# RWKV-7 scan: v and u as one 128-row operand, decay as a diagonal among the keys, transposes of 128 rows

## The chip, the cores and the metric

The kernel runs on one core of a Trainium2 chip. The metric is the device time of one execution, in microseconds (us). The time before is the median of three runs. The engines are PE (matrix products; PEld is its weight load), DVE, ACT and POOL (element-wise work), and SP, whose queue issues most DMAs. PE writes to PSUM, from which ACT and DVE copy to SBUF.

## What is computed

Two requests, of 256 and 1024 tokens, go through two layers with the same weights: a bidirectional RWKV-7 time mixer, a neighbourhood attention, and a squared-ReLU MLP behind each. The change concerns the recurrence of the time mixer alone, for each of 16 heads (of size 64) and both directions:

```python
def step(S, inp):
    r_t, w_t, k_t, v_t, a_t, b_t = inp
    sa = jnp.einsum('bhvk,bhk->bhv', S, a_t)
    S = S * w_t[:, :, None, :] + sa[..., None] * b_t[:, :, None, :] + v_t[..., None] * k_t[:, :, None, :]
    return S, jnp.einsum('bhvk,bhk->bhv', S, r_t)
```

The results of both directions are added, normalised per head, scaled by `lnx_g`, and a bonus (a number per token and head, times v) is added.

## The kernel before

**Stages.** Projections and preparation (up to about 700 us), the scan (up to about 1360), then gate and output product, MLP, attention and MLP. In the preparation, keys and queries of each chunk of 64 tokens are multiplied by running decays and stored in `x_d`, four arrays per direction: b and k (the "keys"), a and r (the "queries"). `dall` keeps each chunk's total decay, and `v_d` the values, token by token.

**The scan by chunks.** 64 tokens are one chunk, so a step of the scan is a handful of 64x64 products in place of 64 steps of the recurrence. A job is 16 chunks of two heads (e = 0, 1, on partitions 0 to 63 and 64 to 127; `HALVES` gives es, the head's own half, and eo, the other one), in both directions d: at step i the forward chunk i and the backward chunk 15 - i are processed together. Ten jobs of 16 steps make 160 steps. Each product below is done for four units (two directions, two heads); in float32 a product takes two PE instructions. Two steps alternate between two sets of PSUM banks.

**The order is written out by hand.** `at(t, f)` puts a piece of work at time t, counted in steps; all pieces are sorted by t and emitted in that order, and PE, ACT, DVE and POOL run them in that order (`manual_schedule`, line 807). Negative times are work for a later job, done beside the steps of the one before it. SP's DMAs are issued in their order too, each when its buffer is free.

**One step** (`scan_step`, line 1016; all its products are recorded at line 1018), with S the state, A, sn, Y and U areas in PSUM:
- s0n, s0a, s0y (about -0.7 to -0.6, so during the step before): what v contributes to the new state, to A and to Y. They need nothing of the state.
- s1y, s1a (0): S times the queries, added to Y and A. s1c (0.1): ACT copies A to `up`.
- s2 (0.3): `up` times the inverse Q, to U. s2c (0.38): ACT copies U to `u`.
- s2b (0.41): the old S is added to sn through a product with the identity.
- s3n, s3y (0.58): what u contributes to the new state and to Y.
- s3c (0.66): ACT copies sn to the new S, multiplied by the chunk's decay, in one instruction per direction (line 1095).
- s4 (1.15): ACT copies Y out (lines 1100, 1103); in the second half of a job, DVE adds it to the other direction's.

So the next step hangs on S - s1a - `up` - s2 - `u` - s3n - S.

**Beside the steps:** `kprod` (line 973) multiplies the keys by the queries, two chunks of both heads a step, into `kps` (two banks, one buffer); next to the queries a, r in the x tile stands an identity (its fifth array), so that the keys come out transposed too. `kcopy` (ACT) takes these as `ll`, `kmask` (DVE) multiplies the rest by a triangular mask as `zz`. `kload` (line 964) loads an x tile (512 KB) from `x_d` into one of eight buffers. `early`, `keep`, `store`, `rank1` (DVE, many small row updates), `merge1`, `merge2` and the `qd` DMAs make the inverse Q of a later job. `vload` loads v of a job. `scan_post` normalises a finished half of a job (DVE, ACT, POOL), transposes it (`tr`, 16 products of 64x64 a half, into two PSUM banks), copies it (`p5`) and stores it to `z_d`.

Of the kernel before, what the change touches and what calls it, by code (L numbers as in the profile page):

```python
# [13 lines left out]
P = 128  # L14
# [4 lines left out]
L = 64  # L19
# [42 lines left out]
class Trunk:  # L62
# [706 lines left out]
    def scan(self):  # L769
# [32 lines left out]
        self.b_x, self.b_y = ([self.pw.tile([P, 512], F32, name=f"{nm}{i}") for i in range(2)] for nm in ("bx", "by"))  # L802
# [16 lines left out]
    def scan_job(self, j):  # L819
# [113 lines left out]
        for n, (d, g) in enumerate(order):  # L933
# [33 lines left out]
            at(2 * n - 10.0, kload)  # L967

        for q in range(16):
# [3 lines left out]
            def kprod(c, g=g, d=d, pr=pr):  # L973
# [3 lines left out]
                for e, (es, eo) in enumerate(HALVES):  # L977
                    for b, out in ((1, eo), (0, es)):
                        w = 128 if b == 0 else 192
                        mm(J["kp"][out, e, 192 * c + 192 - w:192 * c + 192], x[es, b, 2 * pr + c], x[es, 5 - w // 64:5, 2 * pr + c], start=True, stop=True)  # L980

            def kmask(g=g, d=d, pr=pr):
                J["zz", d, g, pr] = z = self.rp.tile([P, 2, 2, P], F32, name="zz", tag="zz", bufs=8)
# [3 lines left out]
            def kcopy(g=g, d=d, pr=pr):  # L987
                J["ll", d, g, pr] = z = self.rp.tile([P, 2, 2, 64], F32, name="ll", tag="ll", bufs=8)
# [3 lines left out]
            for dt, f in ((0.7, lambda f=kprod: f(0)), (0.72, lambda f=kprod: f(1)), (0.95, kmask), (0.74, kcopy)):  # L992
                at(t + dt, f)
# [22 lines left out]
    def scan_step(self, at, J, st, grp, k, i, new, end):  # L1016
# [10 lines left out]
        def banks():  # L1027
            x, y = self.b_x[k % 2], self.b_y[k % 2]
            return pair(x), pair(y), pair(x[:, P:2 * P]), pair(y[:, P:2 * P])
# [23 lines left out]
        def s1a(d, g, c, cc, e, es, eo, yd):  # L1053
            A, Y, sn, U = banks()
            mm(A[es, d], J["x", d, g][es, 2, c], R["S"][es, d], False, True)

        def s1y(d, g, c, cc, e, es, eo, yd):
            A, Y, sn, U = banks()
            mm(Y[eo, yd], J["x", d, g][es, 3, c], R["S"][es, d], False, False)

        def s1c():
            A, Y, sn, U = banks()
# [3 lines left out]
        def s2(d, g, c, cc, e, es, eo, yd):  # L1066
            A, Y, sn, U = banks()
            mm(U[es, d], J["Q"][es, cc, d], R["up"][es, d], False, True)

        def s2b():  # L1070
            A, Y, sn, U = banks()
            S = R["S"]
            if S is None or end:
                return
            for es, eo in HALVES:
                mm(sn[es], self.ident[es, es], S[es], False, False)

        def s2c():
            A, Y, sn, U = banks()
            R["u"] = self.sp.tile([P, 2, 64], F32, name="u", tag="u", bufs=1)  # L1080
            nc.scalar.copy(R["u"], U)

        def s3n(d, g, c, cc, e, es, eo, yd):
            A, Y, sn, U = banks()
            mm(sn[es, d], ll(d, g, c, e)[es], R["u"][es, d], False, True)

        def s3y(d, g, c, cc, e, es, eo, yd):
            A, Y, sn, U = banks()
            mm(Y[eo, yd], zz(d, g, c, e)[es, 64:128], R["u"][es, d], False, True)

        def s3c():
            A, Y, sn, U = banks()
            S = st["S"] = self.sp.tile([P, 2, 64], F32, name="S", tag="S", bufs=2)
            for d, g, c, cc, m, ch in dirs:
                nc.scalar.activation(S[:, d], sn[:, d], AF.Copy, scale=self.dall[:, m, d, ch:ch + 1])

        def s4():
            A, Y, sn, U = banks()
# [12 lines left out]
        if not end:  # L1111
# [912 lines left out]
```

## Time and profile before

| | us |
|---|---|
| time, median of 3 runs (4079.05 to 4081.42) | 4080.91 |
| the profiled execution | 4071.59 |
| its span, first to last instruction | 4069.7 |
| granted TensorE clock, mean of the span | 0.958 |

The profile is of one execution. A row of a group gives line, engine, operation, out<-in by the program's names (`by<-up,qq` is s2, `bx<-u,ll` s3n, `by<-u,zz` s3y, `bx<-S,x` s1a, `bx<-vv,ll` s0n, `by<-vv,zz` s0y, `bx<-S,cst` s2b), the shape, and the count behind x; then busy time and the mean in ns of one; then the idle time of the engine just before, with what ended it. A row of the timeline gives the start and duration in us. A row of a window gives its bounds and length, the busy time (and count) of PE, PEld, DVE, ACT and POOL, the granted clock, the DMA share and GB/s. "Issue" is time in which an engine waited for nothing that the profile shows. A matmul's duration runs to its last result, so those of neighbours overlap.

### The profile page before, as it was taken

To read this page: it belongs to the slowest core of one execution; us is meant where nothing else is said; L and a number is where in the kernel's file an instruction comes from. 1 tells how busy PE (TensorE), PEld (TensorE's weight loads), DVE (VectorE), ACT (ScalarE), POOL (GpSimd) and SP (SyncE) were. 2 spreads that over 40 slices of the span, in tenths; PEclk is the share of its full clock that TensorE was granted. 3 is DMA by queue.
4 is the path that set the end of the run, shared out by engine and by line. 5 is a ranking of instruction groups with operands and counts; after the bars stand their busy time and mean duration, and the time that the engine had idled before them with its cause. 6 is when DMAs were issued, how large, how long until landed. Compare 5 with 4: busy or idle time off the path is not lost.

```text
span 4069.7 us, 87778 instructions
## 1 busy us (share of the span) xinstructions
PE 3719.3 (91%) x35572; PEld 3101.6 (76%) x35572; DVE 2470.3 (61%) x4771; ACT 1538.8 (38%) x3751; POOL 1308.4 (32%) x1256
## 2 busy tenths in 40 slices
PE   7888979677777799999999989999989999999999
PEld 4665659566666688888888879777768788888888
DVE  7898973466666457555555561567664755555555
ACT  6776652354545441111112132556654211112111
POOL 5450001133334434222222250445553422222222
PEclk8997889799999899999999999999989999999999
DMA  3326655866665431011111115233343111111101
GB/s 110 91 83 214 210 190 158 221 182 180 178 172 135 130 111 37 32 42 42 37 37 42 42 62 176 78 89 82 71 117 130 47 42 42 37 37 42 42 32 63
DMA packets 384005, 393.27 MB, mean 97 GB/s; under 512 B 161873, under 2 KB 306481, under 8 KB 382321
## 3 DMA queue, kind: packets, MB, share of 16 engines
q1 hardware_dynamic: 327728, 307.82, 26.3%
q10 hardware_dynamic: 46704, 61.35, 4.4%
q0 software_dynamic: 9168, 18.49, 1.6%
q8 instruction: 279, 4.57, 0.5%
q14 instruction: 126, 1.02, 0.1%
HBM read 277.54 MB, written 121.24 MB: 98 GB/s over the span
## 4 chain that ended last, share of the span: by engine, by line
PE 71%; DVE 12%; issue 5%; ACT 5%; DMA 4%; POOL 2%; SPq 0%; ACTq 0%; DVEq 0%; POOLq 0%
PE ps L108 17%; PE ps L109 17%; PE ps L110 17%; PE by L1018 3%; PE kps L980 3%; PE bx L1018 3%; PE vps L530 1%; PE vps L531 1%; PE vps L532 1%; PE op L1938 1%; DVE mu L199 1%; DVE ll L287 1%; PE pt L1880 1%; DVE cs L646 1%; PE yps L940 1%
## 5 line engine op out<-in xcount | busy, mean ns | idle before, releaser
L1485 DVE TENSOR_TENSOR x<-ps,x 128x256 f32<-128x256 f32 x1488 | 813.1, 595 | 608.5 <-PE ps L110 608.3
L103 POOL TENSOR_TENSOR wlo<-raw,whi 128x1024 fp32r<-128x1024 f32 (+1 forms) x178 | 391.0, 2196 | 857.0 <-ACT whi L102 812.4
L108 PE MATMUL ps<-ahs,whi 128*128 128x512 f32 x1536 | 613.1, 399 | 0.0
L109 PE MATMUL ps<-als,whi 128*128 128x512 f32 x1536 | 599.3, 390 | 0.0
L110 PE MATMUL ps<-ahs,wlo 128*128 128x512 f32 x1536 | 598.9, 390 | 0.0
L108 PE MATMUL ps<-hh,whi 128*128 128x512 f32 (+1 forms) x1536 | 544.1, 354 | 13.5 <-DVE x L1485 13.5
L109 PE MATMUL ps<-hl,whi 128*128 128x512 f32 (+1 forms) x1536 | 543.2, 354 | 0.0
L110 PE MATMUL ps<-hh,wlo 128*128 128x512 f32 (+1 forms) x1536 | 543.1, 354 | 0.0
L102 ACT CAST whi<-raw 128x1024 fp32r<-128x1024 f32 (+1 forms) x206 | 201.4, 978 | 692.6 <-PE ps L109 632.3
L108 PEld LDWEIGHTS ps<-ahs,whi 128*128 128x128 f32 x1536 | 288.9, 188 | 62.2 <-issue 6.9
L110 PEld LDWEIGHTS ps<-ahs,wlo 128*128 128x128 f32 x1536 | 288.4, 188 | 62.0
L108 PEld LDWEIGHTS ps<-hh,whi 128*128 128x128 f32 x1536 | 289.8, 189 | 56.7 <-DVE x L1485 16.6
L1464 POOL TENSOR_TENSOR rl<-rl 128x512 f32<-128x512 f32 (+1 forms) x192 | 174.6, 910 | 489.8 <-PE ps L110 450.5
L109 PEld LDWEIGHTS ps<-als,whi 128*128 128x128 f32 x1536 | 289.0, 188 | 53.1 <-issue 1.0
L110 PEld LDWEIGHTS ps<-hh,wlo 128*128 128x128 f32 x1536 | 289.7, 189 | 40.4
L109 PEld LDWEIGHTS ps<-hl,whi 128*128 128x128 f32 x1536 | 289.7, 189 | 40.1
L1463 ACT ACTIVATE rl<-ps 128x512 f32<-128x512 f32 (+1 forms) x192 | 100.8, 525 | 532.6 <-PE ps L110 532.6
L1466 ACT CAST hh<-rl 128x512 fp32r<-128x512 f32 (+1 forms) x192 | 105.5, 550 | 322.1 <-POOL rl L1464 322.0
L108 PE MATMUL ps<-ahp,whi 128*128 128x256 f32 x768 | 222.9, 290 | 2.2 <-ACT whi L102 1.5
L985 DVE TENSOR_TENSOR zz<-kps,cst 128x512 f32<-128x512 f32 x160 | 110.5, 691 | 179.2 <-ACT ll L990 177.9
L110 PE MATMUL ps<-ahp,wlo 128*128 128x256 f32 x768 | 216.2, 281 | 1.6 <-POOL wlo L103 1.6
L109 PE MATMUL ps<-alp,whi 128*128 128x256 f32 x768 | 215.7, 281 | 0.0
(342 smaller groups left out, 8559.1 us busy)
## 6 DMA issues: line engine op xcount, KB each, us to landing
x<-x_d SPq DMA_DIRECT2D x88, 512.0 KB, 5.7
raw<-in_w_down_dram SPq DMA_DIRECT2D x64, 512.0 KB, 3.1
raw<-in_w_up_dram SPq DMA_DIRECT2D x64, 512.0 KB, 3.3
eab<-x_d SPq DMA_DIRECT2D x80, 256.0 KB, 4.4
x_d<-ar ACTq DMA_DIRECT2D x32, 512.0 KB, 3.0
x_d<-bk ACTq DMA_DIRECT2D x32, 512.0 KB, 3.8
bs<-tab SPq DMA_DIRECT2D x128, 96.0 KB, 4.7
v_d<-vt ACTq DMA_DIRECT2D x80, 128.0 KB, 4.1
```

What stands on the lines that cost most here:

```text
L102: nc.scalar.copy(hi[:, cs], raw)
L103: lo_eng.tensor_tensor(out=lo[:, cs], in0=raw, in1=hi[:, cs].bitcast(F32), op=ALU.subtract)
L108: mm(ps, sh, mh, start=first, stop=False)
L109: mm(ps, sh, ml, start=False, stop=False)
L110: mm(ps, sl, mh, start=False, stop=last)
L980: mm(J["kp"][out, e, 192 * c + 192 - w:192 * c + 192], x[es, b, 2 * pr + c], x[es, 5 - w // 64:5, 2 * pr + c], start=True, stop=True)
L985: nc.vector.tensor_tensor(out=z, in0=src[:, :, :, :P], in1=self.mask[d].unsqueeze(1).unsqueeze(1).to_broadcast([P, 2, 2, P]), op=ALU.mult)
L1018: mm = lambda out, a, b, start, stop: nc.tensor.matmul(out, a, b, start=start, stop=stop, skip_group_check=True)
L1463: nc.scalar.activation(r[:, :n], ps[:, :n], AF.Relu)
L1464: nc.gpsimd.tensor_tensor(out=r[:, :n], in0=r[:, :n], in1=r[:, :n], op=ALU.mult)
L1466: nc.scalar.copy(hh[:, :n], r[:, :n])
L1485: nc.vector.tensor_tensor(out=xv, in0=ps[:, :n], in1=xv, op=ALU.add)
```

## The change

- **One operand for v and u.** A tile `uv` (two buffers, one per four steps) holds u on partitions 0 to 63 and v on 64 to 127. `uvload`, a new DMA of 128 KB per direction and group of four chunks, loads the v part; ACT's copy s2c writes the u part. s0n and s0y are gone: s3n and s3y contract all 128 rows at once. For this the key products put b's results on rows 0 to 63 and k's on 64 to 127 for both heads, and U of both heads lies on partitions 0 to 63, in two banks: `by` becomes one tile of two banks, and head e's U lies in bank e xor (step mod 2).
- **Decay in the keys.** The fifth array of an x tile is no longer a constant identity but the identity times the chunk's decay, made by POOL (`decay`, two instructions for each loaded tile). The transposed keys so carry the decay, s2b multiplies the old S by that diagonal (four products of 64 columns instead of two of 128), and s3c is one plain copy.
- **Transposes.** A finished half is transposed by four 128x128 transposes into one bank, and copied once. The bonus is always added by POOL (`plus`); before, the last job added it on PE.
- **Times and buffers.** Six x tiles instead of eight; `zz` and `ll` have seven buffers instead of eight. `kload` moves from 2n - 10 to 4(n // 2) - 8.5 + n mod 2, `decay` stands at 2n - 6.4, `uvload` at 4(n // 2) - 4.3 (+ 0.1). The first half of the key products moves from 0.7 to 0.45, ahead of s3n; s3y moves behind s3n instead of alternating with it.

```diff
-        grow(self.r_x4, "x4", [P, 5, 4, 64], 8)
-        for t in self.r_x4[0]:
-            for es, eo in HALVES:
-                nc.gpsimd.tensor_copy(t[es, 4], self.ident[es, es].unsqueeze(1).to_broadcast([64, 4, 64]))
+        grow(self.r_x4, "x4", [P, 5, 4, 64], 6)
+        self.r_uv = [[], 0]
+        grow(self.r_uv, "uv", [P, 8, 2, 64], 2)
...
-        self.b_x, self.b_y = ([self.pw.tile([P, 512], F32, name=f"{nm}{i}") for i in range(2)] for nm in ("bx", "by"))
+        self.b_x = [self.pw.tile([P, 512], F32, name=f"bx{i}") for i in range(2)]
+        self.b_y = self.pw.tile([P, 2, 512], F32, name="by")
...
-            at(2 * n - 10.0, kload)
+            def decay(d=d, g=g, m=m, c0=c0):
+                x, w = J["x", d, g], self.dall[:, m, d, c0:c0 + 4]
+                for es, eo in HALVES:
+                    nc.gpsimd.tensor_tensor(out=x[es, 4], in0=self.ident[es, es].unsqueeze(1).to_broadcast([64, 4, 64]),
+                                            in1=w[es].unsqueeze(2).to_broadcast([64, 4, 64]), op=ALU.mult)
+
+            def uvload(d=d, g=g, m=m, c0=c0):
+                if d == 0:
+                    J["uv", g] = self.nxt(self.r_uv)
+                p = g if d == 0 else 3 - g
+                src = self.scr["v_d"][tok(c0), m * P:(m + 1) * P].rearrange("(c s) (e v) -> s c e v", s=L, e=2)
+                nc.sync.dma_start(J["uv", p][64:128, 4 * d:4 * d + 4], src)
+            at(4 * (n // 2) - 8.5 + n % 2, kload)
+            at(2 * n - 6.4, decay)
+            at(4 * (n // 2) - 4.3 + 0.1 * (n % 2), uvload)
...
-                    for b, out in ((1, eo), (0, es)):
-                        w = 128 if b == 0 else 192
+                    for b, (out, _) in enumerate(HALVES):
+                        w = 192 if b else 128
...
-            for dt, f in ((0.7, lambda f=kprod: f(0)), (0.72, lambda f=kprod: f(1)), (0.95, kmask), (0.74, kcopy)):
+            for dt, f in ((0.45, lambda f=kprod: f(0)), (0.72, lambda f=kprod: f(1)), (0.95, kmask), (0.74, kcopy)):
...
+        U = lambda e, d: self.b_y[0:64, e ^ k % 2, P + 64 * d:P + 64 * d + 64]
+        uv = lambda: J["uv", i // 4]
+        place = lambda d: i % 4 if d == 0 else 7 - i % 4
...
-        def s0n(d, g, c, cc, e, es, eo, yd):
-            A, Y, sn, U = banks()
-            mm(sn[es, d], ll(d, g, c, e)[eo], J["v"][eo, cc], d == 0, False)
-
         def s0a(d, g, c, cc, e, es, eo, yd):
-            A, Y, sn, U = banks()
-            mm(A[es, d], zz(d, g, c, e)[eo, 0:64], J["v"][eo, cc], end and d == 0, new)
-
-        def s0y(d, g, c, cc, e, es, eo, yd):
-            A, Y, sn, U = banks()
-            mm(Y[eo, yd], zz(d, g, c, e)[eo, 64:128], J["v"][eo, cc], d == 0, False)
+            A, Y, sn = banks()
+            mm(A[es, d], zz(d, g, c, e)[64:128, 0:64], uv()[64:128, place(d), e], d == 0, new)
...
-            mm(U[es, d], J["Q"][es, cc, d], R["up"][es, d], False, True)
+            mm(U(e, d), J["Q"][es, cc, d], R["up"][es, d], d == 0 and (e == 1 or new), True)
...
-            for es, eo in HALVES:
-                mm(sn[es], self.ident[es, es], S[es], False, False)
+            mm(sn[es, d], J["x", d, g][es, 4, c], R["S"][es, d], False, False)
...
-            R["u"] = self.sp.tile([P, 2, 64], F32, name="u", tag="u", bufs=1)
-            nc.scalar.copy(R["u"], U)
+            src = self.b_y[0:64, :, P:2 * P].rearrange("p b (d v) -> p b d v", d=2)
+            dst = uv()[0:64, i % 4:8 - i % 4:7 - 2 * (i % 4)].rearrange("p d e v -> p e d v")
+            nc.scalar.copy(dst, src[:, ::-1] if k % 2 else src)
...
-            mm(sn[es, d], ll(d, g, c, e)[es], R["u"][es, d], False, True)
+            mm(sn[es, d], ll(d, g, c, e), uv()[:, place(d), e], False, True)
...
-            mm(Y[eo, yd], zz(d, g, c, e)[es, 64:128], R["u"][es, d], False, True)
+            mm(Y[eo, yd], zz(d, g, c, e)[:, 64:128], uv()[:, place(d), e], new and d == 0, True)
...
-            for d, g, c, cc, m, ch in dirs:
-                nc.scalar.activation(S[:, d], sn[:, d], AF.Copy, scale=self.dall[:, m, d, ch:ch + 1])
+            nc.scalar.copy(S, sn)
...
-        if not end:
-            weave(i - 0.6995, s0n)
-        weave(i - 0.6, s0a)
-        weave(i - 0.5995, s0y)
+        weave(i - 0.69, s0a)
...
-        weave(i + 0.5805, s3y)
+        weave(i + 0.59, s3y)
...
+                ps = st["zps"] = self.pa.tile([P, 4, 2, 64], F32, name="zps", tag="aps")
+                for b in range(4):
+                    nc.tensor.transpose(ps[:, b].rearrange("p e t -> p (e t)"), y()[:, b // 2, b % 2 * 2:b % 2 * 2 + 2].rearrange("p c v -> p (c v)"), self.ident)
```

More of the change, by code (lines that the diff above doesn't have):

```diff
@@ L987, in kcopy @@
             def kcopy(g=g, d=d, pr=pr):
-                J["ll", d, g, pr] = z = self.rp.tile([P, 2, 2, 64], F32, name="ll", tag="ll", bufs=8)
+                J["ll", d, g, pr] = z = self.rp.tile([P, 2, 2, 64], F32, name="ll", tag="ll", bufs=7)
                 src = J["kp"][:, :, :384].rearrange("p e (c t) -> p c e t", c=2)
@@ L1120, in scan_step @@
         weave(i + 0.3, s2)
-        at(i + 0.41, s2b)
+        if not new and not end:
+            weave(i + 0.41, s2b)
         at(i + 0.38, s2c)
@@ L1134, in scan_post @@
         nc = self.nc
-        mm = nc.tensor.matmul
         for half in range(2):
@@ L1194, in plus, with tr @@
                 nc.gpsimd.tensor_tensor(out=y(), in0=y(), in1=st["bv"].rearrange("p (x c) v -> p x c v", x=2), op=ALU.add)
[L1196 to L1202 removed]
+            def tr(st=st, y=y):
+                ps = st["zps"] = self.pa.tile([P, 4, 2, 64], F32, name="zps", tag="aps")
+                for b in range(4):
+                    nc.tensor.transpose(ps[:, b].rearrange("p e t -> p (e t)"), y()[:, b // 2, b % 2 * 2:b % 2 * 2 + 2].rearrange("p c v -> p (c v)"), self.ident)
             def p5(st=st, runs=runs):
[L1205 to L1207 removed]
+                zt = self.yp.tile([P, 4, 2, 64], F32, name="zt", tag="zt", bufs=1)
+                nc.scalar.copy(zt, st["zps"])
                 for x, (m, c0) in enumerate(runs):
@@ L1220, in scan_post @@
                     at(t0 + dt, f)
-            if left:
-                at(t0 + 3.3, plus)
-            for i in range(16):
-                at(t0 + when[10] + 0.001 * i, lambda i=i, f=tr: f(i // 4, i // 2 % 2, i % 2))
+            at(t0 + (3.3 if half == 0 or left else 0.66), plus)
+            at(t0 + when[10], tr)
     def rsqrt_x(self, x, pool, n, r):
```

43 lines of the change are left out of this document (14 added, 29 removed).

## The prediction

> **What bounds the kernel now.** I read the page for the span and the shares, then the scan alone, because every line of the diff lies in it.
>
> ```profile
> span 4069.7 us, 87778 instructions
> ...
> PE 3719.3 (91%) x35572; PEld 3101.6 (76%) x35572; DVE 2470.3 (61%) x4771; ACT 1538.8 (38%) x3751; POOL 1308.4 (32%) x1256
> ...
> PE 71%; DVE 12%; issue 5%; ACT 5%; DMA 4%; POOL 2%; SPq 0%; ACTq 0%; DVEq 0%; POOLq 0%
> ```
>
> The page's chain is mostly PE, and 5% of it is "issue": PE waits for nothing that the profile names. The next rows are the uses of the copy `up`, one in each of the 160 scan steps, and the window from the first to the last (PE is its first busy time, its count in brackets; the last numbers are the granted clock, the DMA share and GB/s).
>
> ```profile
> L1064 ACT COPY up<-bx x160: 247/266/297, 755.1 to 1357.7; 128x128 f32<-128x128 f32 x160
> ```
>
> ```profile
> 755.00:1360.00 605.00, 469.52 (x16680) 401.56 (x16680) 390.30 (x938) 311.04 (x1243) 203.77 (x286) 0.95 0.63 166
> ```
>
> So a step takes (1357.7 - 755.1) / 159 = 3.79 us. No engine is full: PE is busy for 470 of 605 us. The waits of PE in this window say where the rest is (us in total, times, longest):
>
> ```profile
> PE by L1018 <- issue: 34.3, 24, 2.7
> PE bx L1018 <- issue: 29.4, 24, 2.9
> ...
> PE aps L850 <- issue: 8.6, 6, 2.5
> ...
> PE kps L980 <- issue: 7.5, 10, 2.5
> PE yps L940 <- issue: 5.8, 6, 2.4
> PE qps L951 <- issue: 4.9, 6, 2.3
> PE zps L1202 <- issue: 2.2, 1, 2.2
> ```
>
> Together 92.7 us in 77 stalls, 1.2 us each, on whatever matmul comes next. I cut the window at three such stalls in a row, and set the instruction queue of the page beside them (packets, MB, share):
>
> ```profile
> 1001.65:1005.59 3.94, 3.20 (x127) 2.65 (x127) 1.50 (x4) 2.46 (x10) 0.00 (x0) 1.00 0.35 110
> 1005.59:1009.88 4.29, 3.65 (x128) 3.00 (x128) 3.42 (x9) 1.76 (x7) 0.00 (x0) 1.00 0.59 152
> 1009.88:1014.37 4.49, 3.40 (x127) 2.67 (x127) 2.39 (x7) 2.55 (x10) 0.00 (x0) 1.00 0.82 255
> ```
>
> ```profile
> q8 instruction: 279, 4.57, 0.5%
> ```
>
> The stalls come every 127 or 128 matmuls with their weight loads. 4.57 MB over the 2 x 35572 PE instructions are 64 bytes each; over 279 packets they are 16 KB, 256 instructions, 128 matmuls. The stalls are PE running out of its program at block ends, and its next block comes about 4 us after the last. **The scan is bound by a dependent chain of about 3.2 us a step, and by the number of PE instructions.** The window is 16680 / 128 = 130 blocks: 512 us of work, 3.94 us each, and 92.7 us of stalls.
>
> The Trainium skill says the contrary in Runtime: NRT & Kernel Launch, Instruction fetch mechanics: the sequencer fetches the next 16 KiB block while it runs the present one, and the crossing is "mostly hidden". The block size agrees with the row above; "hidden" does not agree with 92.7 us at these ends.
>
> The chain itself, in a step without a stall; first ACT, then PE:
>
> ```profile
> 996.01 0.27 ACT L1064 COPY up<-bx 128x128 f32<-128x128 f32 x1
> ...
> 996.90 0.27 ACT L1081 COPY u<-by 128x128 f32<-128x128 f32 x1 [0.45 <-PE by L1018]
> ...
> 997.73 0.52 ACT L1095 ACTIVATE S<-bx,dall 128x64 f32<-128x64 f32 x2
> 998.40 0.37 ACT L990 COPY ll<-kps 128x256 f32<-128x256 f32 x1 [0.16 <-PE kps L980]
> 998.77 0.27 ACT L1064 COPY up<-bx 128x128 f32<-128x128 f32 x1
> 998.93 0.27 ACT L1100 COPY y<-by 128x128 f32<-128x128 f32 x1
> ```
>
> ```profile
> 996.33 0.27 PE L1018 MATMUL by<-up,qq 64*64 64x64 f32 x1
> ...
> 996.44 0.22 PE L1018 MATMUL by<-up,qq 64*64 64x64 f32 x1
> ...
> 996.50 0.22 PE L1018 MATMUL by<-up,qq 64*64 64x64 f32 x1
> ...
> 997.22 0.27 PE L1018 MATMUL bx<-u,ll 64*64 64x64 f32 x1 [0.19 <-ACT u L1081]
> ...
> 997.50 0.83 PE L980 MATMUL kps<-x 64*64 64x128 f32 x16
> 998.11 0.28 PE L1018 MATMUL bx<-S,x 64*64 64x64 f32 x2
> ```
>
> `up` to `up` is 2.76 us. With the end of `up` (996.28) as zero: s2 at 0.05, u 0.62 to 0.89, s3 0.94, S 1.45 to 1.97, the key products' last result 2.05, ll 2.12 to 2.49, `up` 2.49 to 2.76. One pass on a 64x64 quarter of the array takes 0.06 us (996.44 to 996.50), the four quarters side by side. ll, which waits for the 16 key products, stands ahead of `up` on ACT and decides when it starts.
>
> **Part 1: fewer PE instructions.** The rows of what goes or changes:
>
> ```profile
> L1018 PE MATMUL bx<-vv,ll 64*64 64x64 f32 x1152 | 70.7, 238 | 3.0 <-issue 3.0
> L1018 PE MATMUL by<-vv,zz 64*64 64x64 f32 x1280 | 74.1, 229 | 8.1 <-issue 8.1
> L1018 PE MATMUL bx<-S,cst 64*64 64x128 f32 x512 | 54.9, 285 | 0.0
> L1202 PE MATMUL zps<-cst,y 64*64 64x64 f32 x640 | 17.3, 233 | 17.0 <-POOL y L1158 14.8 <-issue 2.2
> ```
>
> s0n (1152) and s0y (1280) go: u and v are one 128-row operand, so s3n and s3y do both. s2b goes from two 128-column products to four of 64 (+512). A half's transposes go from 32 instructions to four, 8 if each has two passes as here (about -430 in the window). Together -2350 of 16680, 112 blocks instead of 130. The array time hardly falls: s0n and s0y ran in quarters that s2 and s0a left free, in the gap before u.
>
> **Part 2: the chain.**
> - s2 now writes all of U to rows 0 to 63, the second head's into the bank (half of the new single tile `by`) from which the previous step's y is copied. No row shows PE waiting for a y copy; the nearest case is that mask product and copy of `kps`, both readers, take turns:
>
> ```profile
> L985 DVE TENSOR_TENSOR zz<-kps,cst 128x512 f32<-128x512 f32 x160 | 110.5, 691 | 179.2 <-ACT ll L990 177.9
> ```
>
>   So I take the wait as real. y ends at 0.16 behind `up` (999.20 against 999.04), so that unit starts at about 0.23 instead of 0.07, and its four passes put u at 0.73 instead of 0.62: +0.11 (0 without the wait, 0.17 if none of it overlaps). Behind it on PE stand s0a, s2b, half the keys and s3; on ACT, u. The Trainium skill's PSUM — Partial Sum Buffer, PSUM bank collisions raise a hardware error, has the rule for it: guard by bank and quadrant, not by address. The zz row agrees.
> - The u copy is now 64 x 256 instead of 128 x 128. ll with 256 columns takes 0.37, u 0.27: +0.10. So s3 starts at 1.16 instead of 0.94.
> - Ahead of s3 the fullest quarter has s0a and s2b, four passes each, and two key passes (0.83 less the last result's 0.3, over four: 0.17 each): 0.8 us, done before u. Half the keys cost nothing here while this holds.
> - s3n and s3y use 128 rows: 0.23 us each, one after the other, where both took 0.28. This changes the array's tiling, twice a step. The rows of such a change elsewhere:
>
> ```profile
> 642.01 0.28 PE L531 MATMUL vps<-wl,mh 128*128 128x256 f32 x1
> 642.13 0.28 PE L532 MATMUL vps<-wh,ml 128*128 128x256 f32 x1
> 642.34 0.45 PE L850 MATMUL aps<-eab 64*64 64x64 f32 x8
> ```
>
>   0.12 from start to start, and 0.21 where 128 rows change to 64: 0.09 each. The change before s3 is hidden (PE waits for u), the one behind s3y is not: the second half of the keys starts at 1.16 + 0.46 + 0.09 = 1.71, and its last result comes at 1.71 + 0.17 + 0.32 = 2.20.
> - S is one copy instead of two scaled ones, 0.27 (as `up`) instead of 0.52, and whole at 1.94 instead of 1.97. It gains nothing: ll still decides, 2.27 to 2.64, and `up` follows at 2.64 instead of 2.49.
>
> So a step without a stall grows by 0.15 us, 24 us over 160; from 0 (no y wait, the tiling change hidden) to 0.3 (both longer).
>
> **Part 3: off the path.** The decay products are 16 POOL instructions a job, on 64 x 256:
>
> ```profile
> L882 POOL COPY mt<-mraw 64x256 f32<-64x256 f32 x40 | 20.8, 627 | 74.7 <-DMA mraw<-dd 58.0 <-issue 16.3
> ...
> x<-x_d SPq DMA_DIRECT2D x88, 512.0 KB, 5.7
> ...
> vv<-v_d SPq DMA_DIRECT2D x16, 256.0 KB, 7.3
> ```
>
> 160 x 0.63 = 101 us on an engine that idles for 401 of 605, each 1.8 to 2.9 steps (5 us or more) ahead of its key product. If that cover is gone, each costs what it is late. The key loads come 1.5 or 0.5 steps later, with six buffers instead of eight, each right behind the last read of its buffer; they still stand 5 steps (some 16 us) before their use, against 5.7 to landing. The uv loads are 8 more DMAs a job on SP's queue, 128 KB each, 3.6 steps (12 us) ahead, against 7.3 for the like. A key load that waits holds up the `eab` loads and `dd` stores behind it on SP; these have some 3 steps of lead. I take nothing; the added traffic can lengthen the fetch of a block, which is in the range. The transposes' 17 us of PE and one of two copies a half shrink: I take 8 us (0 to 17), the identity copies, POOL's alone and before the first step, nothing. The last job's bonus sum goes from PE to POOL, on the tail: +1.
>
> **The sum.** Work is 512 + 24 - 8 = 528 us in 112 blocks, 4.72 us each: 0.78 more than now. A fetch that is late by x today is late by x - 0.78. I take the stalls as spread evenly from 0 to 2.7 us (mean 1.2, longest 2.9): (1.92 / 2.7)^2 = 0.51 of the time stays, on 112 / 130 of the blocks: 92.7 x 0.51 x 0.86 = 41, a gain of 52. In all 24 - 8 - 52 + 1 = -35 us. The profiled execution took 4071.6 us, its span 4069.7; so 4036.6 there. The median of the runs is 9.3 us above that execution, and I carry the difference over: 4080.9 - 35 = **4046 us**. About 0.2% (8 us) is what a measurement of this kernel can tell from no change. Without the y wait the chain grows by 0.04, and the same sum gives 4035, within the forecast.
>
> **The rivals.**
> - *The block is the clock.* If the fetch sets the pace throughout, a block costs 605 / 130 = 4.65 us whatever is in it, and 18 fewer give -84: 3997. For it: the three blocks above, between stalls, take 3.9 to 4.5 us. Against: most of the time is no stall.
> - *The stalls stay.* The rule of Runtime: NRT & Kernel Launch quoted above would leave the stalls to another cause. As a mechanism here: they scale with blocks only (-13), or not at all. Then 24 - 8 - 13 + 1 = +4, 4085; or +17, 4098. Against: their even spacing.
> - *The keys ahead of u wait* (slower). The first half of the keys now stands in front of s3, and `kps` has a single buffer: PE, in order, must wait for zz of the pair before. zz ends 0.4 us into the next step, and PE comes to the keys at about 0.5. The wait of zz for ll (178 us) says that DVE is mostly on time; each 0.5 us that DVE is late, about one of its row updates, moves u's consumers, S and `up`. At +0.5 a step on average (growth 0.65) the work is 608 us, 5.43 a block, the stalls fall to 16, and 104 - 8 - 77 + 1 = +20: 4101. It decides from a growth of about 0.5, where 80 - 8 - 71 + 1 = +2.
>
> **How the numbers follow.** Forecast, 4021 to 4066: 0.48. Block as clock, 3981 to 4020: 0.20. Stalls stay or half of them, 4067 to 4090: 0.14. Slower by the keys' wait, or by stalls that stay whole, over 4090: 0.18. Within 8 us lie some 0.09, from the third; of the rest of that case 0.04 is faster and 0.01 slower. So faster 0.72, same 0.09, slower 0.19. The range for 8 in 10 goes from 3990 to 4100, with about 0.08 left out below and 0.1 above.
>
> **What would show it.** In the profile after: PE instructions about 2400 fewer, "issue" in the scan near 40 us instead of 93; a new wait of PE `by` for ACT y of some 0.1 us a step; the u copy at 0.37; `up` to `up` without a stall 2.9 us. Wrong, if PE waits for DVE zz ahead of the key products, if POOL's decay or a uv load ends PE's waits, or if the stalls no longer come at every 128 matmuls.

## The result, and the profile after

The changed kernel took **4053.9 us** (median of six runs, 4050.7 to 4067.5) against 4080.0 us for the kernel before beside it: ratio 0.9943, interval [0.9927, 0.9959]. A second set of five runs, beside the experiments below, gave 0.9965 [0.9951, 0.9978]. So the change saves 14 to 23 us by these two ratios, where 35 were forecast. The measured 4053.9 lies within the forecast range of 4021 to 4066.

The page of the changed kernel: the span, the engines, the chain of work and the instruction queue.

```profile
span 4065.7 us, 82648 instructions
...
PE 3743.1 (92%) x33028; PEld 3107.9 (76%) x33028; DVE 2508.8 (62%) x4771; ACT 1512.1 (37%) x3587; POOL 1412.1 (35%) x1402
...
q8 instruction: 259, 4.24, 0.5%
...
PE 69%; DVE 14%; ACT 6%; issue 4%; DMA 4%; POOL 3%; SPq 0%; ACTq 0%; DVEq 0%; POOLq 0%
```

PE has 2544 instructions fewer, and 20 fetch packets fewer. Yet PE's busy time is longer, 3743.1 us against 3719.3. This profiled execution, 4067.5 us, is the slowest of its six. Next the uses of `up`, then the scan's window (columns as in the prediction).

```profile
L1074 ACT COPY up<-bx x160: 247/266/283, 764.3 to 1360.0; 128x128 f32<-128x128 f32 x160
```

```profile
755.00:1360.00 605.00, 505.33 (x14392) 420.25 (x14392) 431.36 (x952) 285.74 (x1081) 302.62 (x433) 0.95 0.76 186
```

The scan, first to last `up`, takes 595.7 us instead of 602.6, at the same granted clock of 0.95, and it begins 9.2 us later. The waits of PE in it:

```profile
PE by L1033 <- ACT y L1107: 20.6, 57, 1.0
PE by L1033 <- ACT y L1104: 16.9, 68, 0.7
PE bx L1033 <- issue: 12.0, 9, 2.0
PE kps L995 <- DVE zz L1000: 10.0, 6, 2.0
...
PE by L1033 <- issue: 7.1, 7, 3.2
PE kps L995 <- POOL x L971: 6.1, 5, 1.2
PE kps L995 <- issue: 5.6, 12, 0.8
PE aps L850 <- issue: 2.9, 1, 2.9
...
PE yps L940 <- issue: 1.9, 2, 1.2
```

With two rows of 0.9 and 0.3 us, "issue" is 30.7 us instead of 92.7: the stalls fell by 62. In their place stand waits for the copy of y (37.5 us), for zz and for the decay `x`.

That these stalls are the fetch of the next block can be read from the packets of the instruction queue in the traces. In the scan before lie 131 packets of 16 KB, and 76 of the 77 stalls end 1.1 to 1.7 us after one of them has landed; a moment taken at random in the scan does so in 13% of cases. The distance from one stall to the next is close to a multiple of 127.4 matmuls in 74 of 76 cases. In the changed kernel 23 of 34 stalls end so.

**So the stalls gave 62 us, and other work took most of it back.** Where it went shows in a step without a stall; ACT of the changed kernel (start, duration):

```profile
1014.59 0.27 ACT L1074 COPY up<-bx 128x128 f32<-128x128 f32 x1
...
1015.57 0.37 ACT L1086 COPY uv<-by 64x256 f32<-64x256 f32 x1 [0.55 <-PE by L1033]
...
1016.68 0.27 ACT L1099 COPY S<-bx 128x128 f32<-128x128 f32 x1 [0.59 <-PE bx L1033]
1017.41 0.37 ACT L1005 COPY ll<-kps 128x256 f32<-128x256 f32 x1 [0.46 <-DVE q L901]
1017.71 0.27 ACT L1074 COPY up<-bx 128x128 f32<-128x128 f32 x1
```

and PE of the same step:

```profile
1015.07 0.39 PE L1033 MATMUL by<-up,qq 64*64 64x64 f32 x6 [0.19 <-ACT y L1104]
...
1015.71 0.54 PE L995 MATMUL kps<-x 64*64 64x128 f32 x5
1016.18 0.45 PE L1033 MATMUL bx<-uv,ll 128*64 128x64 f32 x8
1016.47 0.40 PE L1033 MATMUL by<-uv,zz 128*64 128x64 f32 x8
1016.80 0.56 PE L995 MATMUL kps<-x 64*64 64x128 f32 x8
```

With the end of `up` (1014.86) as zero: s2 at 0.21 (before 0.05), u 0.71 to 1.08 (0.62 to 0.89), s3n 1.32 (0.94), the second half of the keys 1.94, ll 2.55 to 2.92 (2.12 to 2.49), `up` 2.85 (2.49). `up` to `up` is 3.12 us instead of 2.76.

### The profile page after: what moved, and what is told of

The parts are those of the page before. It is cut to its first block, busy times and chain, and to the rows that moved or that the text cites. A ratio compares the mean times of both kernels' runs of the same rounds, so it can differ in the third digit from the quotient of the medians.

```text
span 4065.7 us, 82648 instructions
## 1 busy us (share of the span) xinstructions
PE 3743.1 (92%) x33028; PEld 3107.9 (76%) x33028; DVE 2508.8 (62%) x4771; ACT 1512.1 (37%) x3587; POOL 1412.1 (35%) x1402
## 4 chain that ended last, share of the span: by engine, by line
PE 69%; DVE 14%; ACT 6%; issue 4%; DMA 4%; POOL 3%; SPq 0%; ACTq 0%; DVEq 0%; POOLq 0%
PE ps L108 18%; PE ps L109 17%; PE ps L110 17%; PE kps L995 3%; PE bx L1033 2%; PE by L1033 2%; PE vps L530 1%; PE vps L531 1%; PE vps L532 1%; PE op L1933 1%; DVE mu L199 1%; DVE q L901 1%; DVE tmp L899 1%; PE pt L1875 1%; ACT ll L1005 1%
## 5 line engine op out<-in xcount | busy, mean ns | idle before, releaser
L995 PE MATMUL kps<-x 64*64 64x192 f32 (+1 forms) x2560 | 204.9, 330 | 27.9 <-DVE zz L1000 16.2
```

## The experiments

Ratios are against the kernel before on the same chip. "Work" below is the scan less its "issue" waits.

**1. The kernel before without s0n and s0y.** It leaves out what v adds directly to the state and to the output, and shows what the count of instructions alone is worth. (The start flags move to the products that now come first.)

```diff
-        if not end:
-            weave(i - 0.6995, s0n)
         weave(i - 0.6, s0a)
-        weave(i - 0.5995, s0y)
```

> The kernel before without s0n and s0y (v's direct contribution to the new state and to the output is left out), 2432 PE instructions fewer, nothing else moved. Theory (the number of PE instructions is what gains): issue falls from 93 to about 45 us, up to up without a stall stays at 2.76 us, and the time falls by 40 to 55 us, more than by the whole change. Rival (stalls of another cause): issue stays over 80 us, the time within 10 us.

Measured: 4015.6 us, ratio 0.9872 [0.9852, 0.9891], 52 us less.

```profile
L1064 ACT COPY up<-bx x160: 247/265/298, 756.4 to 1307.6; 128x128 f32<-128x128 f32 x160
```

The scan is 551.2 us; 14248 PE instructions in place of 16664; the stalls 47.2 us; work 504.0 against 509.9. Of the 51 us by which the scan is shorter, 45.5 are stalls. PE's busy time falls by 34 us, from 468.4 to 434.5, but little of that was on the path: work falls by 6. So the gain is mostly fetch, not array time, and the theory holds.

**2. The y copy ahead of the next `up`.**

```diff
-        at(i + 1.15, s4)
+        at(i + 0.67, s4)
```

> The changed kernel with one edit: ACT copies y right behind the new S (time 0.67) instead of behind up (1.15), so that s2 no longer meets it in the bank of U. Theory (the y wait is the largest part of what the chain gained): the waits of PE by for ACT y, 38.5 us in the changed kernel's trace, go to under 5 us, up to up without a stall falls from 3.12 to about 2.97 us, and the time falls by 15 to 25 us against the changed kernel (ratio to the kernel before near 0.989). Rival (the array work ahead of u is the limit, or the stalls take it back): the waits go, the time moves by under 6 us.

Measured: 4045.2 us, ratio 0.9941 [0.9927, 0.9956]: 1 us less than the first set of the changed kernel, 10 less than run 5. The scan is 580.3 us. PE's waits for y fall from 37.5 to 1.1 us, but those for `up` rise from 1.2 to 14.3, and a clean step is 3.06 us. ACT and then PE in such a step:

```profile
950.10 0.27 ACT L1074 COPY up<-bx 128x128 f32<-128x128 f32 x1
...
952.26 0.27 ACT L1104 COPY y<-by 128x128 f32<-128x128 f32 x1
952.75 0.37 ACT L1005 COPY ll<-kps 128x256 f32<-128x256 f32 x1 [0.22 <-PE kps L995]
953.16 0.27 ACT L1074 COPY up<-bx 128x128 f32<-128x128 f32 x1
```

```profile
952.14 0.56 PE L995 MATMUL kps<-x 64*64 64x128 f32 x8
952.58 0.27 PE L1033 MATMUL by<-S,x 64*64 64x64 f32 x1
```

Counted from the end of `up` at 950.37, s2 starts 0.16 us earlier than in the changed kernel, and s3n and ll 0.17; but `up` comes at 2.79 instead of 2.85. The edit moved the y wait more than it removed it. The next step's first product of S, which writes `by`, now starts 0.05 us behind the end of the earlier y copy, and 0.21 us behind the last key product; in the changed kernel 0.05 us lie between these two products. In 119 of the 160 steps it starts so, 0.04 to 0.05 us behind y. The list of waits doesn't show this, because the key products' durations reach past it. So the time comes out near the rival's, but what a step without any y wait takes, with the keys where they are, no run shows; 3.12 less 0.17 would be 2.95, an estimate from these rows and near the theory's 2.97.

**3. The decay as one 128-row POOL instruction** (with a stacked identity `idf`) in place of two of 64 rows.

```diff
-                for es, eo in HALVES:
-                    nc.gpsimd.tensor_tensor(out=x[es, 4], in0=self.ident[es, es].unsqueeze(1).to_broadcast([64, 4, 64]),
-                                            in1=w[es].unsqueeze(2).to_broadcast([64, 4, 64]), op=ALU.mult)
+                nc.gpsimd.tensor_tensor(out=x[:, 4], in0=self.idf.unsqueeze(1).to_broadcast([P, 4, 64]),
+                                        in1=w.unsqueeze(2).to_broadcast([P, 4, 64]), op=ALU.mult)
```

> The changed kernel with the decay product of a tile in one POOL instruction on 128 rows instead of two on 64 (a stacked identity made once). Theory (POOL's decay slows DVE beside it: DVE's row updates have a mean of 434 and 401 ns in the scan, against 360 and 351 before, and 660 while ten decay products ran in a row before the first step): POOL's decay falls from 107 to about 54 us, the DVE rows to about 395 and 375 ns, and the time by 5 to 15 us. Rival (DVE is off the path, its rows are slower for nothing): the rows get faster, the time stays within 4 us.

Measured: 4054.1 us, ratio 0.9959 [0.9944, 0.9975], between the two of the changed kernel: no effect that can be told. POOL's time for it halves (74 instructions of 685 ns in the scan instead of 148 of 676), and the scan begins at 758.7. Of DVE's two row updates one falls from a mean of 433 to 407 ns and the other stays, 402 and 405, where 395 and 375 were expected. As the time is the same, the rival is nearer.

**4. Sixteen PE instructions more in a step**, eight matmuls of one column each, where PE waits for y.

```diff
+        def pad():
+            for n in range(8):
+                es, eo = HALVES[n % 2]
+                mm(self.b_x[(k + 1) % 2][es, 300 + n:301 + n], self.ident[64:128, 64:128], self.one[64:128], True, True)
+        at(i + 0.25, pad)
```

> The changed kernel with 8 more products of one column a step (16 PE instructions, 2560 in all, about as many as the change took out), put where PE waits for y before s2; results that nothing reads. Theory (PE runs out of its program at block ends, so that instructions cost by their number): issue in the scan rises from 31 to 60 or more us, and the time by 25 to 45 us, back to the kernel before. Rival (the stalls have another cause): issue stays near 31 us, and the time rises by 0 to 16 us for the array time alone.

Measured: 4120.2 us, ratio 1.0121 [1.0095, 1.0147]. The stalls rise to 54.6 us, as more blocks must; but the scan grows to 653.6, more by work (599.0 against 556 to 565) than by stalls. The direction is that of the theory. But PE is busy for 577 us of the scan instead of 492 to 498, and the granted clock over it is 0.91 in this profile, against 0.95 and 0.97 in the two of the changed kernel. So the size proves little.

**5. The changed kernel again, with a second profile.**

> The changed kernel once more, beside the three kernels below. It is to give the reference that they are compared with: 0.991 to 0.996 of the kernel before. If the lost 9 us ahead of the scan's first `up` belong to the change, the first `up` stands again near 764 us; if they belong to that one execution, near 755 to 759, as in the run with an earlier y copy.

```profile
L1074 ACT COPY up<-bx x160: 247/265/286, 761.8 to 1344.3; 128x128 f32<-128x128 f32 x160
```

4055.4 us, ratio 0.9965 [0.9951, 0.9978]. The same program takes 582.5 us for the scan here, at a granted clock of 0.97, and 595.7 in the first profile, at 0.95: one profile alone can't carry a difference of 10 us. The start is 6.7 us later than before, so the late start belongs to the change.

**6. All keys behind s3n again.**

```diff
-            for dt, f in ((0.45, lambda f=kprod: f(0)), ...
+            for dt, f in ((0.7, lambda f=kprod: f(0)), ...
```

> The changed kernel with all key products behind s3n again. Theory (half the keys ahead of u cost about what they gain): s3n starts about 1.15 us behind `up` instead of 1.32, but the last key result comes later, ll still at about 2.55, a clean step of 3.1 to 3.2 us; PE no longer waits for zz ahead of the keys (16 us fall to under 3); the time within 8 us of the changed kernel. Rival (the array work ahead of u is what lengthens the step): a clean step of 2.9 to 3.0 and 10 to 25 us less. Second rival (the half ahead of u really hides key work): a clean step of 3.3 and 10 to 25 us more.

Measured: 4052.4 us, ratio 0.9950 [0.9938, 0.9963], the same as run 5. A clean step:

```profile
889.51 0.27 ACT L1074 COPY up<-bx 128x128 f32<-128x128 f32 x1 [0.46 <-PE bx L1033]
...
892.46 0.37 ACT L1005 COPY ll<-kps 128x256 f32<-128x256 f32 x1 [0.79 <-PE kps L995]
892.76 0.27 ACT L1074 COPY up<-bx 128x128 f32<-128x128 f32 x1
```

```profile
890.91 0.45 PE L1033 MATMUL bx<-uv,ll 128*64 128x64 f32 x8
```

s3n starts 1.13 us behind `up` instead of 1.32, as u allows it; so the half ahead of u does delay s3n. But ll comes at 2.68 instead of 2.55, and a clean step is 3.25 us: on balance the half ahead of u shortens the step, by 0.13. That would make 20 us over 160 steps, and the time shows none of it: in the scan the stalls fell from 26.2 to 18.1 us against run 5, and PE's waits for zz from 7.3 to 0.9, which together are 14 to 15 us. The second rival had the mechanism right, and the theory the time.

**7. Run 2 and run 3 together.** Edits as there.

> The changed kernel with the y copy ahead of the next `up` and the decay as one 128-row instruction. Theory (ll is what `up` waits for, so most of what the y wait gives is taken back, and the decay costs little): a clean step of about 3.05 us, 5 to 15 us less than the changed kernel. Rival (the y wait and the decay are each a full cost on the path): 38 us of y wait and more go, 25 to 45 us less.

Measured: 4049.0 us, ratio 0.9943 [0.9931, 0.9956]; clean step 3.07, scan 585.6, stalls 41.4. 6 us less than run 5, at the lower end of the theory, with intervals that overlap. The first products of S wait for the y copy here as in run 2, so this run doesn't show a step without it either.

**8. Run 7 with all keys behind s3n and ll behind the next `up`.**

```diff
-            for dt, f in ((0.45, lambda f=kprod: f(0)), (0.72, lambda f=kprod: f(1)), (0.95, kmask), (0.74, kcopy)):
+            for dt, f in ((0.7, lambda f=kprod: f(0)), (0.72, lambda f=kprod: f(1)), (1.14, kmask), (1.12, kcopy)):
```

> The run above with all keys behind s3n and the copy ll behind the next `up` on ACT. Theory (`up` stands late because ll stands ahead of it): a clean step of 2.75 to 2.9 us instead of 3.05, PE waits for ACT up fall; with less work to a block the stalls rise from about 35 to 50 us; the net is 10 to 30 us less than the run above. Rival (a late ll holds the single key buffer, so the next keys wait for zz and ll): the wait moves to the key products, PE waits for ACT ll or DVE zz ahead of kps by 20 us or more, and the time is that of the run above or longer.

Measured: 4045.9 us, ratio 0.9932 [0.9920, 0.9945]: 10 us less than the changed kernel on the same chip, the best version found, though a clean step is still 3.09 us. A step of it, `up` first, then PE:

```profile
882.54 0.27 ACT L1076 COPY up<-bx 128x128 f32<-128x128 f32 x1 [0.85 <-PE bx L1035]
...
884.27 0.27 ACT L1101 COPY S<-bx 128x128 f32<-128x128 f32 x1 [0.39 <-PE bx L1035]
...
885.63 0.27 ACT L1076 COPY up<-bx 128x128 f32<-128x128 f32 x1 [0.85 <-PE bx L1035]
```

```profile
884.39 0.72 PE L997 MATMUL kps<-x 64*64 64x128 f32 x14
884.88 0.23 PE L1035 MATMUL bx<-S,x 64*64 64x64 f32 x1
```

ll no longer stands ahead of `up`: `up` waits 0.85 us for PE. S is whole at 884.54, but PE is in the keys until 884.9, and the next step's products of S stand behind them. PE's own order is now the limit. Neither theory had this.

**9. One more ACT copy on the chain of the kernel before.** No PE instruction more.

```diff
-            nc.scalar.copy(R["up"], A)
+            up0 = self.sp.tile([P, 2, 64], F32, name="up0", tag="up0", bufs=1)
+            nc.scalar.copy(up0, A)
+            nc.scalar.copy(R["up"], up0)
```

> The kernel before with one more ACT copy (0.27 us) between `bx` and `up` in each of the 160 steps: no PE instruction more, 43 us more on the chain. Theory (a fetch that is late by x is late by less where a block holds more work; over the runs so far the stalls of a block were 0.71 us at 3.92 us of work, 0.42 at 4.55, 0.24 at 4.99, 0.16 at 5.11): the work of a block rises from 3.92 to 4.25 us, its stalls fall to about 0.56, all stalls from 93 to about 73; the scan is about 23 us longer, ratio 1.004 to 1.008. Rival (stalls depend on the number of instructions alone): stalls stay near 93 and the scan is 43 us longer, ratio 1.0105. Second rival (the block is the clock): no change.

Measured: 4070.4 us, ratio 1.0012 [0.9998, 1.0025]: 5 us by the ratio, 0 to 10 by its interval.

```profile
L1065 ACT COPY up<-bx x160: 245/265/300, 756.4 to 1367.3; 128x128 f32<-128x128 f32 x160
L1066 ACT COPY up<-up x160: 297/298/299, 756.7 to 1367.6; 128x128 f32<-128x128 f32 x160
```

160 copies of 298 ns are 48 us on the chain, and the scan grows by 8.3, since the stalls fall from 92.7 to 62.5. The kernel before hardly feels its chain; the result lies between the theory and "the block is the clock".

**10. The transposes of the kernel before in the changed one.**

```diff
-                for b in range(4):
-                    nc.tensor.transpose(ps[:, b].rearrange("p e t -> p (e t)"), ...
+                rows, out = HALVES[h][0], HALVES[par][0]
+                nc.tensor.matmul(st["zps"][h ^ par][out, b], y()[rows, b // 2, b % 2 * 2 + par], self.ident[rows, rows], start=True, stop=True)
...
-                nc.scalar.copy(zt, st["zps"])
+                for x in range(2):
+                    nc.scalar.copy(zt[:, x], st["zps"][x])
```

> The changed kernel with the transposes of the kernel before (16 pairs of 64x64 instructions and two copies for half a job, in place of 4 pairs of 128x128 and one copy). Prediction's term (the new transposes save 8 us): 8 us more than the changed kernel, so 0.997 to 0.999 of the kernel before. Theory now (they save nothing, since PE waits there for POOL and for the copy zt): within 4 us of the changed kernel; PE waits for ACT zt at 8 to 10 us in both.

Measured: 4061.1 us, ratio 0.9982 [0.9969, 0.9995]. That is 7 us more than run 5 (0.9965) and 16 more than the first set (0.9943), not measured beside these, and with intervals that overlap in the first case. The prediction's 8 us fit better than none. Array time is the same, 14.1 us against 13.8 in the scan; what differs there are 504 PE instructions more, 4 blocks, and 36 ACT copies of 0.38 us instead of 18 of 0.59. The run doesn't part the two.

**11. s3n and s3y as two products of 64 rows each.** The halves with v go where s0n and s0y were, and s2b goes ahead of s2. (A first form, with the halves with v right ahead of s3n, gave no time.)

```diff
+            mm(sn[es, d], ll(d, g, c, e)[64:128], uv()[64:128, place(d), e], False, False)
...
-            mm(sn[es, d], ll(d, g, c, e), uv()[:, place(d), e], False, True)
+            mm(sn[es, d], ll(d, g, c, e)[0:64], uv()[0:64, place(d), e], False, True)
...
-            weave(i + 0.41, s2b)
+            weave(i + 0.29, s2b)
```

> The changed kernel with each 128-row product of s3n and s3y as two of 64 rows; the halves with v go ahead of the next `up`, where the kernel before had them, and s2b ahead of s2. The y wait, the u copy of 64x256, the decay and the half of the keys ahead of u stay; 2432 PE instructions come back. Theory (128-row products run one after the other, where the quarters run side by side: 0.6 us for both against 0.3 for the halves with u; and a block takes its work or the fetch, whichever is longer, 4.6 to 4.7 us at under 4.3 us of work): s3n and s3y together 0.3 us, a clean step of 2.85 to 2.95 us instead of 3.13; work about 4.0 us in 130 blocks, so 4.65 us a block: the scan 604 us, about 20 longer than the changed kernel's 582 to 596, stalls back at 70 to 95; ratio 0.998 to 1.003. Rival (the array form costs nothing on the path): clean step 3.1 and the time of the changed kernel plus 40 us, ratio over 1.005. Second rival (the count of instructions doesn't matter): 30 to 40 us shorter than the changed kernel, ratio 0.987.

Measured: 4115.6 us, ratio 1.0107 [1.0089, 1.0125]. The number is the rival's, but the mechanism is neither's: a clean step is 3.44 us, and the stalls are only 36.2.

```profile
894.80 0.33 PE L1033 MATMUL bx<-uv,zz 64*64 64x64 f32 x4
894.92 0.33 PE L1033 MATMUL bx<-uv,ll 64*64 64x64 f32 x4
```

Four such instructions start in 0.12 us, two in a pass of 0.06; on four quarters it would be eight. In this layout v lies on rows 64 to 127 for both heads, and u on 0 to 63, so a product of a half uses two quarters at most. So here two products of half the rows came out dearer than one of 128 rows, though the new place of s2b may have its part in that. The run doesn't price the 128-row form against the four quarters of the kernel before, as it was meant to; that stays open.

**12. The copy of run 9 in the changed kernel.**

> The changed kernel with one more ACT copy (0.27 us) between `bx` and `up` in each of the 160 steps, as was done to the kernel before, where it cost 5 us of the 43. Theory (a block costs the longer of its work and the fetch; the changed kernel has 5.0 us of work in a block, so the fetch hides little more): the work of a block rises to about 5.35 us, the stalls fall from 26 to 31 us to about 15, and the scan is 25 to 40 us longer than the changed kernel's; ratio 1.001 to 1.006. Rival (the chain isn't what a step waits for, in either kernel): 0 to 10 us longer, ratio 0.995 to 0.998, with the waits of PE for ACT up risen by as much as those for ACT y and the stalls fell.

Measured: 4078.3 us, ratio 1.0011 [0.9999, 1.0024]: 19 us more than run 5 (0.9965), 28 more than the first set (0.9943), of 48 on the chain; the same copy cost 5 before, at most 10 by the interval. The scan is 611.0 us, the stalls 12.9, and the waits for y more than double:

```profile
PE by L1033 <- ACT y L1109: 43.9, 64, 1.5
PE by L1033 <- ACT y L1106: 43.5, 77, 1.0
```

So the change moved the bound: the time of the kernel after follows its step more than that of the one before does.

**All scans side by side**, from one profile each: scan from first to last `up`, blocks as PE instructions between these divided by 128, stalls as the sum of PE's "issue" rows, work as the scan less the stalls.

| kernel | scan, us | blocks | stalls, us | work a block | stalls a block | time a block |
|---|---|---|---|---|---|---|
| before | 602.6 | 130.2 | 92.7 | 3.92 | 0.71 | 4.63 |
| before, longer chain (9) | 610.9 | 130.2 | 62.5 | 4.21 | 0.48 | 4.69 |
| before, no s0n, s0y (1) | 551.2 | 111.3 | 47.2 | 4.53 | 0.42 | 4.95 |
| 16 instructions more (4) | 653.6 | 131.2 | 54.6 | 4.57 | 0.42 | 4.98 |
| s3 in halves (11) | 637.0 | 130.2 | 36.2 | 4.61 | 0.28 | 4.89 |
| old transposes (10) | 598.0 | 115.3 | 38.5 | 4.85 | 0.33 | 5.19 |
| keys back, ll behind `up` (8) | 580.2 | 111.7 | 34.9 | 4.88 | 0.31 | 5.19 |
| y early (2) | 580.3 | 111.4 | 35.9 | 4.89 | 0.32 | 5.21 |
| y early, one decay (7) | 585.6 | 111.4 | 41.4 | 4.89 | 0.37 | 5.26 |
| one decay (3) | 588.3 | 111.4 | 35.2 | 4.97 | 0.32 | 5.28 |
| after (5) | 582.5 | 111.4 | 26.2 | 4.99 | 0.24 | 5.23 |
| after, first profile | 595.7 | 111.4 | 30.7 | 5.07 | 0.28 | 5.35 |
| keys back (6) | 587.8 | 111.4 | 18.1 | 5.12 | 0.16 | 5.28 |
| after, longer chain (12) | 611.0 | 111.4 | 12.9 | 5.37 | 0.12 | 5.49 |

Stalls and work trade against each other: from 3.92 to 5.37 us of work a block, time a block rises by 0.86 us for 1.45. Rows close together scatter by 0.1. The granted clock differs too: it was 0.91 in the scan of run 4, 0.93 in run 1, 0.94 in run 9, and 0.95 to 0.97 in the others. The trade fits with variants whose clean steps differ by 0.1 to 0.2 us and that end within 10 us of each other.

## Why the prediction was right

- **Fewer instructions, fewer stalls: right.** The scan has 2408 PE instructions fewer (2350 said), 111 blocks (112). Run 1 shows by itself that this count is worth some 45 us, with 6 us less work beside it, and the packets of the instruction queue show that the stalls are fetches. The stall model, by which a fetch late by x is late by less where a block holds more work, gave 41 us at 4.72 us of work, 0.37 a block; the table has 0.28 to 0.42 around it. The true work was higher, so the stalls fell further, to 26 to 31.
- **"The scan is bound by a dependent chain": too strong for the kernel before.** Run 9 put 48 us on it and lost 5. The sum counted a longer chain fully and took a part of it back through the stalls; in run 9 work rises by 38 us and the stalls fall by 30.
- **The y wait: real, rightly sized.** u was to come at 0.73 and comes at 0.71. It isn't the second head's unit alone that waits but all of s2: its first product starts at 0.21.
- **The u copy: right**, 0.37.
- **"Half the keys cost nothing here", and "the change before s3 is hidden": the step that failed.** s3 was to start at 1.16, and starts at 1.32. The key products themselves run about as predicted: the last one starts at 1.07, and u is whole at 1.08. But the first product of 128 rows follows the last key product by 0.25 us, in 141 steps of that trace, so the change of tiling that was to hide behind u shows. With the keys behind (run 6) s3n starts 0.05 us after u, at 1.13. Running on: the second half of the keys at 1.94 (1.71 said), `up` at 2.85 (2.64), a clean step of 3.12 us (2.91). The chain term is +0.36 instead of +0.15.
- **The tiling change: nearly right.** s3n to the second half of the keys takes 0.62 us; 0.55 was said.
- **"The array time hardly falls": it rises.** PE's busy time in the window goes from 469.5 to 505.3 us. Work is 556 to 565 us, against 510 before and 528 predicted: 28 to 37 us lost here and in the step above, 10 to 15 regained in the stalls.
- **POOL's decay off the path: mostly right.** 148 of them in the scan take 100 us as said. But PE waits 6.1 us for `x`, and the decays slow DVE (last section), which may be part of PE's wait of 10.0 us for zz. The prediction named both waits as signs that it is wrong; they came, but small. Halving the decays (run 3) changes nothing that can be told.
- **Transposes −8: not contradicted** (run 10), though not through array time, which stayed at 13 to 14 us.
- **Start-up at nothing: wrong.** The first `up` stands at 755.1 us before (756.4 in runs 1 and 9), at 758.8 to 764.3 in the eight profiles with the decay in two instructions, and at 757.1 to 758.7 in the three with one. The chain that leads to it in the changed kernel holds nine row updates of DVE of 0.66 to 0.69 us beside ten decays in a row, and 0.33 to 0.35 right behind these. The last slow one and the first fast one, then the decays:

```profile
752.62 0.68 DVE tmp L899
753.33 0.33 DVE q L901
```

```profile
746.36 6.76 POOL L971 TENSOR_TENSOR x<-cst,dall 64x256 f32<-64x256 f32 x10
```

  That is about 3 us of the 7 to 9; in run 3 four of them take 0.55 to 0.58. The rest stays open.
- **The rivals.** The block as clock would have had 518 us in the scan; it had 583 to 596, and the kernels of the table show 4.63 to 5.49 us a block. Stalls that stay: they fell by two thirds. Keys that wait for zz: it happens, 10.0 us in 6 waits, not 0.5 us a step.

In sum: −62 to −66 us of stalls (−52 said), +46 to +55 of work (+16 said), +7 to +9 at the start in these two profiles (0 said). The remainder behind the scan differs by 6 to 12 us between these profiles (2712.0 us before; 2705.7 and 2700.4 after) in work that the change doesn't touch, beyond the last job's bonus sum, and isn't credited to it: two variants of the kernel before have 2711.1 (run 1) and 2701.6 (run 9) there. Up to the end of the scan these two profiles thus show +2 and −13 us, where the sum said −36. They are the slowest and the fastest execution of their sets. That the time lies within the range is in part luck: the mechanism of the stalls was right, the work was undercounted by some 30 us, and the further fall of the stalls, the width of the range and the time behind the scan made up for it.

## What to carry to other kernels

Where an engine's stalls come at equal counts of instructions, cut instructions first, and expect a chain beside them to be nearly free: add a dummy copy to the chain and see whether the time moves. Once the count is cut, the step itself binds, and every product that is put ahead of a critical one on an engine that works in order has to be counted up to the critical one's start, tiling changes included. When an edit takes a wait away, look for the next instruction that waits for the same one: it may only have moved, and it may stand in no list. And a product that is wider by stacking two operands gave up running its parts side by side here: s3n and s3y took 0.28 us together, and take 0.62 up to the next key product. Here fewer instructions cost array time.

## What the runs showed of the hardware that was not expected

**DVE runs slower beside POOL.** DVE in the step above, then POOL:

```profile
1015.30 0.35 DVE L899 TENSOR_TENSOR tmp<-mt,q 128x192 f32<-128x192 f32 x1
...
1016.07 0.63 DVE L899 TENSOR_TENSOR tmp<-mt,q 128x175 f32<-128x175 f32 x1
```

```profile
1015.87 1.32 POOL L971 TENSOR_TENSOR x<-cst,dall 64x256 f32<-64x256 f32 x2 [7.50 <-PE bx L1033]
```

The smaller operation takes 0.63 us where it runs beside the two decays, the larger one 0.35 just ahead of them. Over the whole window (before, then after):

```profile
L901 DVE TENSOR_TENSOR q<-q,tmp 128x255 f32<-128x255 f32 (+14 forms) x248 | 89.4, 361 | 8.5
L899 DVE TENSOR_TENSOR tmp<-mt,q 128x240 f32<-128x240 f32 (+14 forms) x247 | 86.8, 351 | 5.3
```

```profile
L901 DVE TENSOR_TENSOR q<-q,tmp 128x192 f32<-128x192 f32 (+14 forms) x255 | 110.3, 433 | 8.8
...
L899 DVE TENSOR_TENSOR tmp<-mt,q 128x192 f32<-128x192 f32 (+14 forms) x255 | 102.4, 402 | 5.5
```

The Trainium skill states it in SBUF — State Buffer, Who interferes with whom: a DVE instruction with two SBUF inputs and a POOL instruction that reads SBUF contend for a shared port pair, and this pair is an exclusive lock. These rows agree that they contend. That one waits for the whole of the other they don't show: in the same trace 25 decays with no DVE work beside them take 0.60 to 0.61 us, so that taking turns with updates of 0.33 us would need 0.94 us a pair, and in the run of ten a decay takes 0.68 and an update 0.67 at the same time. DVE's means grow by 72 and 51 ns. The prediction counted POOL's 100 us as free without looking at DVE's inputs.

**An ACT copy from SBUF took longer than from PSUM.** In run 9 the same 128x128 copy takes 265 ns from `bx` (PSUM) and 298 ns from `up0` (SBUF).

**A fetch hides behind work in part only.** The "mostly hidden" of the Trainium skill (Runtime: NRT & Kernel Launch, Instruction fetch mechanics) comes true only toward the end of the table: 0.12 us a block at 5.37 us of work, 0.71 at 3.92.
